# TensorE's order in the S5 part written out, with projection products between each unit's own

## The chip, the cores and the metric

The kernel runs on one core of a Trainium2 chip. Five engines work beside each other, each through its own queue and in order: TensorE (PE, with its weight loads PEld), VectorE (DVE), ScalarE (ACT), GpSimd (POOL) and SyncE (SP), which in this kernel issues nearly all DMAs. The metric is the device time of one execution in microseconds (us); the median of three executions of the kernel before is 683.53 us (682.38 to 684.18).

## The reference, cut to what matters

One layer over 1024 prompt tokens and 32 sample tokens (8 sequences of 4). The normalised input `a` is multiplied by `w_in`; the columns of the product feed an mLSTM group and an S5 group, whose outputs are joined, projected, and passed through two further stages of products.

```python
a = rmsnorm(h, ln_mix)
x_m, z_m, o_m, i_pre, f_pre, x_s, z_s = split(a @ w_in)   # 512 columns each, the gates 4 + 4
# mLSTM group: conv(x_m), q/k/v, gates i and f, chunkwise scan over the tokens, times sigmoid(o_m), silu(z_m)
# S5 group: 32 channel groups of 16 with a 64-dim complex diagonal state each
bu = einsum(x_s, Bbar); xs = associative_scan(a, bu)      # along the tokens
y  = Re(C xs) + D x_s;  y = gelu(y)
y  = y * sigmoid(y @ w_glu + b_glu) * silu(z_s)
h  = h + concat(hA, y) @ w_out
h  = h + sigmoid(h @ w_ple_gate) * rmsnorm(p @ w_ple);  out = rmsnorm(h, ln_final)
```

The change touches only the order in which `x_s`, `o_m`, `z_s` and the S5 units' products are made; what is computed stays the same.

## The kernel before, in words

All large products are made of three matmuls each (leading part times leading part, and two with a remainder: L116 to L118, in `mm3`). A projection of 128 columns of `w_in` over all 1056 tokens is `mtile`: for each of three token ranges (256, 384 and 416 tokens, `CH`) it runs 8 steps of three matmuls into one of two PSUM tiles of the tag `mm`, and then evacuates that tile. `s5_x(j, c)` does so for the j-th quarter of `x_s` (four quarters), and after the last range writes the quarter to DRAM (`d_us`, eight DMAs). `o_tile` does one token tile of `o_m` (8 steps of three 256-column matmuls); `o_rest` does the second half of `o_m`, which is eight such tiles and 64 small matmuls for the sample rows. `z_tile` is a projection for `z_m` or `z_s` with a tanh and a DVE product behind it, written to `d_z`. Weights come by `wtile`: a raw tile (two buffers), a leading part (three buffers) and a remainder (three), shared by all projections in the order of the program.

Order of the program: tokens are normalised and transposed, with the first half of `o_m` and quarter 0 of `x_s` between (up to 64 us of the profile); DVE prepares the S5 tables (L316 to L487); quarters 1 to 3 of `x_s`; then the eight S5 units, u = 0..7. A unit has two parts. `s5_mats(u)` prepares its matrices: DVE products `wtr`, `wti`; four transposes on TensorE (`tpW`, L514); the tile `WV`; `cs` from GpSimd products and DVE sums; four matmuls `kp` (L538); then `ks`, which goes to DRAM (`dK`) and comes back skewed as `tz`; and rotation tables on GpSimd. `s5_run(u)` runs it: the quarter's tokens `us` from `d_us`; eight matmuls `vr` and `vi` (L574) from `WV` and `us`; four products, two sums, four scans and six more products on DVE (L578 to L603), which give `xs_`; eight matmuls `py` (L609 from `tz` and `us`, L610 from `cs` and `xs_`); the GELU on ACT and DVE, with the result in `y2` and `ysm`; and eight DMAs of `y2` to `d_y`. After the units comes `s5_final`, and the buffers of the S5 part are closed (`s5x.close()`); the buffers of the mLSTM part are opened in the same place later. Then the mLSTM gates (a chain of small DVE operations, two transposes and four DMAs), the `x_m` projections with their convolution, the rest of `o_m`, the `z` projections and the four mLSTM heads, the GLU, and the output and gate products.

What sets the order: the engines take their queues in order, and the queues are laid out when the program is built, by a planner that goes through a simulated time. Of the instructions whose inputs are ready in that time it takes the one with the best priority; priority is the place in the program, and `tc.high_priority()` lifts it. In the kernel before all eight units stand in one `tc.high_priority()` block, so that a unit's products go ahead of any projection as soon as the planner sees them ready, and projections (also of later parts of the program) fill what is left, on every engine.

Of the kernel before, what the change touches and what calls it, by code (L numbers as in the profile page):

```python
# [8 lines left out]
F32 = mybir.dt.float32  # L9
# [14 lines left out]
CH = ((0, 256), (256, 384), (640, 416))  # L24
LOC = tuple((c, 128 * (i - b)) for i, (c, b) in enumerate(((0, 0),) * 2 + ((1, 2),) * 3 + ((2, 5),) * 4))
# [3 lines left out]
def tile_hymba(ctx: ExitStack, tc: tile.TileContext, d: dict, o: list):  # L29
# [27 lines left out]
    # ------------------------------------------------------------------ phase 1  # L57
# [67 lines left out]
    # ---------------- normalised input, transposed, in two parts  # L125
# [18 lines left out]
    def x_tile(i, xt):  # L144
# [8 lines left out]
        else:  # L153
            # the first tile in halves
# [19 lines left out]
    def mtile(hi, lo, evac, name, cs=(0, 1, 2)):  # L174
        for c in cs:
            t0, n = CH[c]
            ps = pm([128, 416], f"ps_{name}")
            for k in range(8):
                mm3(ps[:, :n], hi[:, k, :], lo[:, k, :], aTh[c][:, k, :n], aTl[c][:, k, :n], k == 0, k == 7)
            with tc.high_priority():  # L180
                evac(c, t0, n, ps)

    # ------------------------------------------------------------------ gates and output gate (token major)
# [15 lines left out]
    def o_tile(hh, ws, i):  # L199
        n = NH[hh]  # L200
# [3 lines left out]
        for k in range(8):  # L204
            hi, lo = ws[k // 4]
            mm3(ps[:m, :n], aTh[c][:, k, off:off + m], aTl[c][:, k, off:off + m],
                hi[:, k % 4, :], lo[:, k % 4, :], k == 0, k == 7)
        with tc.high_priority():
# [8 lines left out]
            if hh == 0:  # L217
                V.tensor_tensor(gates[:m, :, i], ps[:m, 256:264], bgr[:m], op=ADD)  # L218

    def o_rest():  # L220
        # the second half; its sample rows with the column blocks of w side by side in the array
# [12 lines left out]
        for j in range(4):  # L234
            p0 = 32 * (2 + j // 2)
            A.activation(sos[p0:p0 + 32, 64 * (j % 2):64 * (j % 2) + 64], ps[32 * j:32 * j + 32], AF.Tanh, scale=0.5)
        for i in range(8):
            o_tile(1, ws, i)
# [7 lines left out]
    def s5_x(j, c):  # L246
        if c == 0:
# [14 lines left out]
        mtile(*xsw[j], evac, "xs", (c,))  # L262
# [24 lines left out]
    # small parameters: rows -> columns by one transpose  # L287
# [26 lines left out]
    # ------------------------------------------------------------------ S5  # L314
# [44 lines left out]
    # bases e^{i theta 2^l}, l = 1..9, and rho = |a|^8  # L359
# [19 lines left out]
    # powers a^0 .. a^8 : [128, 16, 9]  # L379
# [12 lines left out]
    k = 1  # L392
# [4 lines left out]
    # rotation tables: fine A = E^1..E^8, coarse Bt = E^0, E^8, .., E^120 with E = e^{8 i theta}  # L397
# [16 lines left out]
    # input matrices times the ZOH factor  # L414
# [1053 lines left out]
```

## Time and profile before

| | |
|---|---|
| median of three timed executions | 683.53 us (682.38 to 684.18) |
| span of the profiled execution (first to last instruction) | 678.6 us |
| time of the profiled execution beyond its span | not given by the page |
| PE busy | 621.7 us, 92% of the span |
| DVE busy | 451.6 us, 67% |
| ACT, POOL busy | 252.2 us, 256.4 us |
| mean granted TensorE clock | 0.982 of full speed |
| chain that ended last, by engine | PE 56%, DVE 26%, DMA 6%, issue 5% |

The page gives busy time as a share of the whole span, so that 92% on PE is an average over stages with different limits. A busy time is the union of the instructions' own times; a matmul's time holds its way through the array (0.28 us for a product that the next one follows after 0.12 us), so that short waits between matmuls don't show as idle. The granted clock has two levels, 1.00 (2.4 GHz) and 0.50 (1.2 GHz); numbers between are means over a stretch.

### The profile page before, as it was taken

What the parts mean: (1) busy time and instruction counts of PE and PEld (TensorE: products, weight loads), DVE (VectorE), ACT (ScalarE), POOL (GpSimd) and SP (SyncE); (2) the same over time, 40 slices, a digit from 0 to 9 for tenths busy, and PEclk for the clock granted to TensorE, in tenths of its full rate; (3) what the DMA queues carried; (4) which work ended last, traced back from release to release, by engine and by line L of the source; (5) the groups of instructions that cost most, each with busy time, mean ns of one, the idle gap of its engine ahead of it and who ended that gap; (6) DMA issues with size and microseconds to landing.
All of it is one profiled execution on the core that took longest, in us unless ns stands there. A gap on an engine that the chain in (4) does not pass through costs nothing.

```text
span 678.6 us, 11611 instructions
## 1 busy us (share of the span) xinstructions
PE 621.7 (92%) x4068; PEld 543.6 (80%) x4068; DVE 451.6 (67%) x1257; ACT 252.2 (37%) x623; POOL 256.4 (38%) x269
## 2 busy tenths in 40 slices
PE   3998996987888897999999998999999999999995
PEld 2997995776767896899898978867888877788885
DVE  4779758999999966358678579966222324566435
ACT  5553331232232346314445253555111324443332
POOL 5712347665565126243533246583011203001000
PEclk9999998999979999999999998999999999999998
DMA  8804341153325366225345373577541246313111
GB/s 279 233 32 98 112 129 51 47 130 93 88 58 129 82 165 213 64 75 156 114 154 151 101 195 133 170 256 233 185 144 42 94 162 237 140 32 124 56 70 62
DMA packets 109679, 86.34 MB, mean 127 GB/s; under 512 B 33263, under 2 KB 92547, under 8 KB 109622
## 3 DMA queue, kind: packets, MB, share of 16 engines
q1 hardware_dynamic: 109622, 85.61, 41.9%
q8 instruction: 32, 0.52, 0.3%
q14 instruction: 25, 0.20, 0.1%
HBM read 60.10 MB, written 25.49 MB: 126 GB/s over the span
## 4 chain that ended last, share of the span: by engine, by line
PE 56%; DVE 26%; DMA 6%; issue 5%; ACT 3%; POOL 2%; SPq 1%; DVEq 0%; POOLq 0%; ACTq 0%
PE po L1287 5%; PE po L1289 4%; PE po L1288 4%; PE po L1396 4%; PE po L1398 4%; PE po L1397 4%; PE ps_zs L116 2%; PE ps_zs L117 2%; PE ps_zs L118 2%; DVE cs L533 2%; DVE cs L526 1%; SPq L35 1%; DVE zr L590 1%; DVE u L373 1%; PE pe L1377 1%
## 5 line engine op out<-in xcount | busy, mean ns | idle before, releaser
L1396 PE MATMUL po<-wgh,hTh 128*128 128x512 f32 (+1 forms) x136 | 52.1, 383 | 0.0
L1398 PE MATMUL po<-wgh,hTl 128*128 128x512 f32 (+1 forms) x136 | 51.5, 379 | 0.0
L1397 PE MATMUL po<-wgl,hTh 128*128 128x512 f32 (+1 forms) x136 | 51.4, 378 | 0.0
L116 PE MATMUL ps_o<-hi_o,aTh 128*128 128x264 f32 (+2 forms) x136 | 41.0, 302 | 0.7 <-ACT aTh L171 0.7
L117 PE MATMUL ps_o<-lo_o,aTh 128*128 128x264 f32 (+2 forms) x136 | 40.2, 296 | 1.4 <-POOL lo_o L112 1.4
L118 PE MATMUL ps_o<-hi_o,aTl 128*128 128x264 f32 (+2 forms) x136 | 40.4, 297 | 0.0
L116 PE MATMUL ps_xs<-aTh,hi_xs 128*128 128x256 f32 (+2 forms) x96 | 32.3, 337 | 2.5 <-DVE gates L218 2.5
L116 PE MATMUL ps_xm<-aTh,hi_xm 128*128 128x256 f32 (+2 forms) x96 | 33.8, 352 | 0.0
L116 PE MATMUL ps_zs<-aTh,hi_zs 128*128 128x256 f32 (+2 forms) x96 | 32.2, 335 | 0.7 <-DVE ztmp L666 0.7
L1287 PE MATMUL po<-woh,mh 128*128 128x512 f32 x80 | 32.6, 408 | 0.0
L117 PE MATMUL ps_xm<-aTl,hi_xm 128*128 128x256 f32 (+2 forms) x96 | 32.4, 338 | 0.0
L118 PE MATMUL ps_xs<-aTh,lo_xs 128*128 128x256 f32 (+2 forms) x96 | 32.1, 334 | 0.0
L118 PE MATMUL ps_zm<-aTh,lo_zm 128*128 128x256 f32 (+2 forms) x96 | 32.0, 334 | 0.0
L118 PE MATMUL ps_xm<-aTh,lo_xm 128*128 128x256 f32 (+2 forms) x96 | 32.0, 333 | 0.0
L117 PE MATMUL ps_xs<-aTl,hi_xs 128*128 128x256 f32 (+2 forms) x96 | 31.8, 332 | 0.0
L1288 PE MATMUL po<-wol,mh 128*128 128x512 f32 x80 | 31.8, 397 | 0.0
L118 PE MATMUL ps_zs<-aTh,lo_zs 128*128 128x256 f32 (+2 forms) x96 | 31.8, 331 | 0.0
L1289 PE MATMUL po<-woh,mlo 128*128 128x512 f32 x80 | 31.8, 397 | 0.0
L116 PE MATMUL ps_zm<-aTh,hi_zm 128*128 128x256 f32 (+2 forms) x96 | 31.7, 331 | 0.0
L117 PE MATMUL ps_zm<-aTl,hi_zm 128*128 128x256 f32 (+2 forms) x96 | 31.7, 330 | 0.0
L117 PE MATMUL ps_zs<-aTl,hi_zs 128*128 128x256 f32 (+2 forms) x96 | 31.5, 328 | 0.0
L1296 DVE TENSOR_TENSOR hTl<-tr,hTh 128x512 fp32r<-128x512 f32 x16 | 11.0, 690 | 30.3 <-ACT hTh L1295 30.1
(587 smaller groups left out, 2043.4 us busy)
## 6 DMA issues: line engine op xcount, KB each, us to landing
xt<-in_x_prompt SPq DMA_DIRECT2D x15, 512.0 KB
Wraw<-in_w_out SPq DMA_DIRECT2D x16, 256.0 KB
Wraw<-in_w_ple_gate SPq DMA_DIRECT2D x16, 256.0 KB
d_h<-xt SPq DMA_DIRECT2D x8, 512.0 KB
h_t<-d_h SPq DMA_DIRECT2D x8, 512.0 KB
out<-g_t SPq DMA_DIRECT2D x14, 256.0 KB
mt<-d_m SPq DMA_DIRECT2D x10, 256.0 KB
d_us<-xs SPq DMA_DIRECT2D x32, 72.0 KB
```

The costliest lines, as they stand in the source:

```text
L35: nc.sync.dma_start(out, in_)
L116: T.matmul(ps, wh, xh, start=first, stop=False)
L117: T.matmul(ps, wh, xl, start=False, stop=False)
L118: T.matmul(ps, wl, xh, start=False, stop=last)
L533: V.scalar_tensor_tensor(cs[64:128, g2:4:2], u1[ph], -1.0, u2[ph], op0=MUL, op1=SUB)
L1287: T.matmul(ps, mh[:, k % 4, :], hi, start=k == 4, stop=False)
L1288: T.matmul(ps, mh[:, k % 4, :], lo, start=False, stop=False)
L1289: T.matmul(ps, mlo[:, k % 4, :], hi, start=False, stop=k == 3)
L1296: V.tensor_tensor(hTl[i][:, 4 * q:4 * q + 4, :], tp, hi.bitcast(F32), op=SUB)
L1396: T.matmul(ps[:, :b - a], hTh[i][:, k, :], hi[:, ws], start=k == 4, stop=False)
L1397: T.matmul(ps[:, :b - a], hTh[i][:, k, :], lo[:, ws], start=False, stop=False)
L1398: T.matmul(ps[:, :b - a], hTl[i][:, k, :], hi[:, ws], start=False, stop=k == 3)
```

## The change

Inside the block `with tc.manual_schedule(engines={PE})` TensorE's instructions keep the order in which they are written; the other engines' queues are laid out as before. To write that order, the functions of the units and of the projections become generators that stop at given points. `take(cols)` runs on through `filler()`, which makes quarters 1 to 3 of `x_s`, then `o_rest`, then two of the four `z_s` projections, until so many matmul columns have been written (it stops at the first step boundary at or past the number). `prod` runs a unit's generator to its next stop, at high priority. `o_rest()` and `zs_tile(0)`, `zs_tile(1)` leave their old places behind the mLSTM gates. The order for each unit is: `vr`/`vi`, `kp`, 18,000 columns of filler, `py`, 2,400 columns, the next unit's `tpW`, 2,400 columns. The diff also drops comments.

```diff
+FILL_A, FILL_B, FILL_C = 18000, 2400, 2400
-    def mtile(hi, lo, evac, name, cs=(0, 1, 2)):
+    def mtile_g(hi, lo, evac, name, cs=(0, 1, 2)):
         for c in cs:
             t0, n = CH[c]
             ps = pm([128, 416], f"ps_{name}")
             for k in range(8):
                 mm3(ps[:, :n], hi[:, k, :], lo[:, k, :], aTh[c][:, k, :n], aTl[c][:, k, :n], k == 0, k == 7)
+                if k < 7:
+                    yield 3 * n
             with tc.high_priority():
                 evac(c, t0, n, ps)
+            yield 3 * n
...
     def o_rest():
...
+        yield 1200
         for i in range(8):
-            o_tile(1, ws, i)
+            yield from o_tile_g(1, ws, i)
...
     def s5_mats(u):
         cmul(V, wtr, wti, ...)
+        yield
         tp = pt([128, 4, 128], "tpW")
...
+        yield WV
         kp = pt([128, 128], "kp")
...
         cmul(G, rtr, rti, ...)
-        return WV, cs, tz, rtr, rti
+        yield cs, tz, rtr, rti
-    def s5_run(u, mats):
-        WV, cs, tz, rtr, rti = mats
+    def s5_run(u, WV, get):
...
                     T.matmul(v_[ph, q, :], WV[:, x, q, ph], us[:, 2 * q + g2, :], start=True, stop=True)
+        yield
+        cs, tz, rtr, rti = get()
...
         A.copy(fin[:, 2 * q0:2 * q0 + 4], xs_[:, :, 136])
+        yield
+        pys = []
         for q in range(2):
             ps = pn([128, 2, 136], "py")
+            pys.append(ps)
...
+        yield
+        for q, ps in enumerate(pys):
             sq = s5.tile([128, 2, 136], F32, tag="sq", name="sq", bufs=2)
...
-    for j in range(1, 4):
-        xsw.append(xs_w(j))
-        for c in range(3):
-            s5_x(j, c)
-    with tc.high_priority():
-        for u in range(8):
-            mats = s5_mats(u)
-            s5_run(u, mats)
-    s5_final()
-    s5x.close()
...
+    def filler():
+        for j in range(1, 4):
+            xsw.append(xs_w(j))
+            for c in range(3):
+                yield from s5_x_g(j, c)
+        yield from o_rest()
+        for j in range(2):
+            yield from z_tile_g(2056 + 128 * j, 4 + j, f"zs{j}")
+    fill = filler()
+    def take(cols):
+        for n in fill:
+            cols -= n
+            if cols <= 0:
+                break
+    def prod(gen):
+        with tc.high_priority():
+            return next(gen)
+    with tc.manual_schedule(engines={mybir.EngineType.PE}):
+        mats = [s5_mats(u) for u in range(8)]
+        prod(mats[0])
+        WV = prod(mats[0])
+        take(3000)
+        for u in range(8):
+            run = s5_run(u, WV, lambda: parts)
+            prod(run)
+            parts = prod(mats[u])
+            prod(run)
+            if u < 7:
+                prod(mats[u + 1])
+            take(FILL_A)
+            prod(run)
+            take(FILL_B)
+            if u < 7:
+                WV = prod(mats[u + 1])
+                take(FILL_C)
+            prod(run)
+        s5_final()
+        for _ in fill:
+            pass
+    s5x.close()
...
     xmc[0] = mtile_xm(0)
-    o_rest()
     xmc[1] = mtile_xm(1)
...
     zm_tile(1)
-    zs_tile(0)
-    zs_tile(1)
     glu_w()
```

## Rows read from the trace of the kernel before

**Rows 1.** Busy time by stretch: stretch, length, then busy us and instructions of each engine

```profile
core 0: us, PE busy (x) PEld busy (x) DVE busy (x) ACT busy (x) POOL busy (x), PEclk, DMA share, GB/s
63.70:94.90 31.20, 28.74 (x178) 28.13 (x176) 21.43 (x120) 11.53 (x35) 9.66 (x8) 0.95 0.46 133
94.90:232.90 138.00, 114.27 (x881) 98.94 (x879) 132.97 (x295) 36.57 (x120) 84.47 (x98) 0.95 0.34 85
232.90:300.00 67.10, 62.91 (x414) 59.40 (x415) 37.23 (x92) 27.31 (x60) 24.10 (x17) 1.00 0.48 132
300.00:445.00 145.00, 138.13 (x1018) 128.70 (x1018) 113.16 (x388) 66.81 (x169) 64.88 (x61) 0.99 0.48 147
445.00:678.60 233.60, 226.48 (x1223) 179.06 (x1222) 102.33 (x182) 77.32 (x182) 44.46 (x45) 0.99 0.38 129
```

**Rows 2.** Timeline of PE at 64 us: start, duration, instruction, idle before it

```profile
63.75 0.27 PE L460 MATMUL tpC<-ident,cn 128*128 128x128 f32 x1
66.59 0.39 PE L116 MATMUL ps_xs<-aTh,hi_xs 128*128 128x256 f32 x1 [2.46 <-DVE gates L218]
```

**Rows 3.** Timeline of DVE, the last table operation and the first unit's first two

```profile
79.61 0.29 DVE L377 TENSOR_TENSOR rBi<-cu,cu 128x128 f32<-128x128 f32 x1
89.83 0.40 DVE L372 TENSOR_TENSOR u<-pwr,Bbr 128x256 f32<-128x256 f32 x1
90.16 0.41 DVE L373 TENSOR_TENSOR u<-pwi,Bbi 128x256 f32<-128x256 f32 x1
```

**Rows 4.** Waits of DVE from 79 to 95 us: waiter, releaser, total, times, longest

```profile
DVE xs L249 <- DMA er<-ends: 4.0, 1, 4.0
DVE rw L711 <- PE tpr L710: 3.3, 1, 3.3
DVE M__2437 L731 <- DMA mp<-mc: 2.3, 1, 2.3
```

**Rows 5.** Timeline of PE around the first unit's products

```profile
103.08 0.43 PE L538 MATMUL kp<-cs,Bs 128*32 128x128 f32 x8
103.44 0.71 PE L574 MATMUL vr<-us,WV 128*64 128x144 f32 x8
104.57 0.46 PE L117 MATMUL ps_xs<-aTl,hi_xs 128*128 128x416 f32 x1
...
105.05 0.35 PE L116 MATMUL ps_xs<-aTh,hi_xs 128*128 128x416 f32 x1
105.24 0.35 PE L117 MATMUL ps_xs<-aTl,hi_xs 128*128 128x416 f32 x1
...
106.73 0.38 PE L514 MATMUL tpW<-ident,wtr 128*128 128x128 f32 x2
106.95 0.38 PE L514 MATMUL tpW<-ident,wti 128*128 128x128 f32 x2
```

**Rows 6.** Timeline of PE: half of unit 1's py, and unit 7's first and last products

```profile
138.90 0.47 PE L609 MATMUL py<-us,tz 128*128 128x136 f32 x2
139.90 0.38 PE L514 MATMUL tpW<-ident,wtr 128*128 128x128 f32 x2
214.46 0.70 PE L574 MATMUL vr<-us,WV 128*64 128x144 f32 x6
232.29 0.40 PE L610 MATMUL py<-xs__2316,cs 128*128 128x136 f32 x2
```

**Rows 7.** Groups of PE from 63.7 to 232.9 us, by line

```profile
L116 PE MATMUL ps_xm<-aTh,hi_xm 128*128 128x256 f32 (+2 forms) x48 | 17.0, 354 | 0.0
L116 PE MATMUL ps_zm<-aTh,hi_zm 128*128 128x256 f32 (+1 forms) x12 | 3.7, 308 | 0.0
L941 PE MATMUL vps<-wv,xm 128*128 128x128 f32 x16 | 2.1, 275 | 0.0
```

**Rows 8.** Busy time in stretches at the low and at the full clock

```profile
114.90:121.50 6.60, 5.91 (x36) 4.74 (x37) 6.59 (x17) 0.27 (x1) 4.12 (x5) 0.50 0.25 71
147.00:166.40 19.40, 13.96 (x117) 12.16 (x115) 19.12 (x38) 5.72 (x18) 11.49 (x14) 1.00 0.55 134
196.80:203.40 6.60, 6.60 (x33) 4.42 (x33) 6.60 (x7) 0.27 (x1) 6.60 (x5) 0.50 0.01 2
```

**Rows 9.** Waits of PE from 94 to 230 us

```profile
PE tps L754 <- DVE colv L746: 5.5, 1, 5.5
PE py L610 <- DVE xs__1676 L603: 2.9, 1, 2.9
```

**Rows 10.** Timeline of SP (DMA issues) in unit 6, and PE's wait for what they bring

```profile
204.46 3.83 SPq L35 DMA_DIRECT2D d_y<-y  x8
208.39 0.52 SPq L35 DMA_DIRECT2D dK<-ks  x1
210.98 0.62 SPq L35 DMA_DIRECT2D tz<-dK  x1
216.72 0.47 PE L609 MATMUL py<-us,tz 128*128 128x136 f32 x2 [1.56 <-DMA tz<-dK]
```

More of the change, by code (lines that the diff above doesn't have):

```diff
@@ L179, in mtile @@
                 mm3(ps[:, :n], hi[:, k, :], lo[:, k, :], aTh[c][:, k, :n], aTl[c][:, k, :n], k == 0, k == 7)
+                if k < 7:
+                    yield 3 * n
             with tc.high_priority():
                 evac(c, t0, n, ps)
+            yield 3 * n
+    def mtile(hi, lo, evac, name, cs=(0, 1, 2)):
+        for _ in mtile_g(hi, lo, evac, name, cs):
+            pass
     NH = (264, 256)
@@ L199, in o_tile, with o_tile_g @@
     def o_tile(hh, ws, i):
+        for _ in o_tile_g(hh, ws, i):
+            pass
+    def o_tile_g(hh, ws, i):
         n = NH[hh]
@@ L207, in o_tile @@
                 hi[:, k % 4, :], lo[:, k % 4, :], k == 0, k == 7)
+            if k < 7:
+                yield 3 * n
         with tc.high_priority():
@@ L218, in o_tile @@
                 V.tensor_tensor(gates[:m, :, i], ps[:m, 256:264], bgr[:m], op=ADD)
+        yield 3 * n
     def o_rest():
@@ L246, in s5_x, with s5_x_g @@
     def s5_x(j, c):
+        for _ in s5_x_g(j, c):
+            pass
+    def s5_x_g(j, c):
         if c == 0:
@@ L260, in evac @@
                 A.copy(xs[:, 4:8, 136:144], v)
-        mtile(*xsw[j], evac, "xs", (c,))
+        yield from mtile_g(*xsw[j], evac, "xs", (c,))
         if c == 2:
@@ L621, in s5_run @@
                 y2[16 * t:16 * t + 16].rearrange("c g (k n) -> c (g k) n", n=32))
+        yield
     def s5_final():
@@ L647, in s5_final, with z_tile_g @@
         dma(o_pim[0, 0], ob[:, 64:128])
-    for j in range(1, 4):
-        xsw.append(xs_w(j))
-        for c in range(3):
-            s5_x(j, c)
-    with tc.high_priority():
-        for u in range(8):
-            mats = s5_mats(u)
-            s5_run(u, mats)
-    s5_final()
-    s5x.close()
     def z_tile(c0, idx, name):
+        for _ in z_tile_g(c0, idx, name):
+            pass
+    def z_tile_g(c0, idx, name):
         hi, lo = wtile(wcols(c0, 128), 8, 128, name)
@@ L667, in evac @@
             dma(d_z[idx, :, t0:t0 + n], tz_[:, :n])
-        mtile(hi, lo, evac, name)
+        yield from mtile_g(hi, lo, evac, name)
+    def filler():
[36 more added lines that the diff above has]
+        for _ in fill:
+            pass
+    s5x.close()
     SC = 128.0 ** -0.5
```

## The prediction

> **What bounds the kernel now.** I read four views in this order. The busy times by stretch come first, because the change lies in one stretch: from 94.9 to 232.9 us, where the S5 units run, DVE is busy for 132.97 of 138.0 us and PE for 114.27; from 300 us on PE is at 95% or more [rows 1]. So the units' stretch is set by DVE, nearly all that follows by PE. The reader is to see that PE's 23.7 idle us there are the room that a better order can use, and that DVE's work is not made less by any order on PE. Second, PE's timeline at the units: the first unit's `vr` starts at 103.44, unit 7's at 214.46, and the last `py` ends at 232.7 [rows 5, 6]; that is (214.46 - 103.44) / 7 = 15.9 us a unit. Third, DVE's timeline ahead of the first unit: the S5 tables are finished at 79.9, but the first unit's products start at 89.83 [rows 3]; between 79 and 95 us DVE waits for 9.6 us in all, for a transpose and two small DMAs of the mLSTM gates, which stand in its queue ahead of the unit [rows 4]. Fourth, what PE does there: after a wait of 2.46 us it starts on quarter 1 of `x_s` at 66.59 [rows 2], and with quarters 1 to 3 it is busy for 28.7 of the 31.2 us up to 94.9 [rows 1].
>
> **The change, part by part.** Columns first: quarters 1 to 3 of `x_s` are 3 x 8 x 3 x 1056 = 76,032, `o_rest` counts 1,200 + 8 x 8 x 3 x 256 = 50,352, two `z_s` projections 50,688; together 177,072. At 0.19 us for 416 columns (105.05 to 105.24, [rows 5]), 0.457 ns each, that is 81 us of PE.
>
> *What is uncovered.* PE's written order begins with the first unit's `tpW`, which needs DVE's first products. The quarters that fill PE from 66.6 us today stand behind it, so PE has only a few transposes between 64 and about 82 us: some 16 us of idle PE. That costs nothing at once, as DVE works on the tables until 79.9; it takes 16 us out of PE's room, and those must come back in the units.
>
> *Start of the units.* Tables done at 79.9 [rows 3]; six products at 0.33 us apart (89.83 to 90.16, [rows 3]) 2.0; `tpW` 4 x 0.11 = 0.44 (106.73 to 106.95 for two, [rows 5]); `take(3000)` four steps, 3,072 columns, 1.4. PE comes out of a long idle; the 5.5 us wait for `colv` [rows 9] ended at the granted clock 0.50, which then held from 114.9 to 121.5 [rows 8], so I double the last two, 3.7. First `vr`: 79.9 + 2.0 + 3.7, some 86 with the hand-overs, against 103.4. Bounds: 84 at the full clock; 95.6 if the gates' 9.6 us of DVE waits come back ahead of the unit. I take 86: with `x_s` off PE and its `d_us` DMAs later, the transposes and DMAs of that chain have less ahead of them.
>
> *The period of a unit.* DVE alone: 15.9 us, as before. PE alone: 22,800 columns, and about half a step more at each of three stops (steps are 768 to 1,248 columns), say 24,300 x 0.457 = 11.1; `vr`/`vi` 1.13 (103.44 to 104.57), `kp` 0.36, `tpW` 0.44 [rows 5], `py` 2 x 1.0 (138.90 to 139.90, [rows 6]): 15.0. The two are nearly alike, and in a fixed order each waits for the other's lateness. The new wait is `py` behind 18,000 columns: queued behind `py` stand all the filler, `tpW` and the next `vr`, on which DVE depends. What `py` waits for is `xs_` and `tz`. `tz` comes by SP: eight `d_y` DMAs of the unit before, then `dK`, then `tz`: 204.46 to 208.39, 2.6 us until `tz` is issued, and PE has it 5.7 us after that [rows 10], 12.2 us in all. If that chain starts with `vr`, `py` runs at 12.2, and the next `vr` comes 2.0 + 1.3 + 0.44 + 1.3 = 5.0 us later (two blocks of about 2,900 columns): 17.2. Ends: 15.9 (DVE alone; `tz` early) and 19.7 (the chain 2.5 us late). I take 17.0, nearest to the row of the chain. New DVE work in this stretch, the six evacuations of `z_s`, leaves the stretch that follows by as much and is inside the 1.1 us over 15.9.
>
> *The last unit.* 18.2 us before, from `vr` to the end of `py` [rows 6]. The filler lasts (177,072 - 3,072) / 24,300 = 7.2 units, so unit 7 has little beside it; with 12.2 for `tz`, 2.0 for `py` and a little for `xs_`, 15. Ends 13 and 18.
>
> *End of the units:* 86 + 7 x 17.0 + 15 = 220, against 232.7: 12.7 us earlier.
>
> *What is left for later.* `z_s` 0 and 1 take the place of `x_m` 0 and 1, 48 steps each [rows 7], the same columns. Not done by then, and done before: 12 steps of `z_m` (36 matmuls, some 10,800 columns, 4.9 us) and 16 `vps` [rows 7], 2.1 us at 0.13 each: 7 us of PE. Against it unit 7 leaves PE about 9 us free, in which the projection `x_m` 0 may start, as it is outside the written order, if its weights are there; I count 3. Net 4 us later, ends 0 and 7. After that the same work is queued: ten projections (9.6 before) to lay beside four mLSTM heads, on a PE that is 94% to 97% busy [rows 1]; I take it at the same pace.
>
> *Sum:* -12.7 + 4 = -8.7 us on the span of 678.6, 669.9. The median of the runs is 4.9 us above that span (the page gives no other time for the profiled execution); I carry this over: 674.8, say 675.
>
> **A rule of the skill against it.** The rows show both: the 5.5 us wait [rows 9] was followed by the clock 0.50 [rows 8], the 2.9 us wait in unit 2 [rows 9] was not: 147.0 to 166.4 ran at 1.00 [rows 8]. The Trainium skill, "TensorE: Matmul & The Clock Gate", section "HAM oscillation — how this bites in real kernels", says that a loop whose every pass waits for a transfer between its bursts of matmuls starts every pass at the low clock. [...] It is the first rival.
>
> **The rivals.** *Low clock in each unit.* If every unit loses the clock for 6.6 us, as at 114.9 and 196.8 [rows 8], PE needs 15.0 + 3.3 = 18.3 a unit and sets the period: 86 + 128 + 15 = 229, -3.6 + 4: 684, no change. For it: PE waits in each unit by my own period. Against: these waits are 2 us, and the trace's 2.9 us cost no clock. The page named above has this as a rule; the price is the rows' alone.
>
> *`tz` rules, and it is late (slower).* The written order fixes `py` 18,000 columns after `kp`, 8.2 us; before, PE took other work until `tz` came. If `ks` or the `d_y` DMAs ahead of it on SP are 2.5 us later than I count, the period is 19.5: 86 + 136.5 + 15 = 237.5, +4.8 + 4 us: 692. It decides from a period of 18.2 us on, where the sum is zero: 86 + 7 x 18.2 + 15 + 4 = 232.4. For it: unit 6 waited for `tz` even with 18 us between `kp` and `py`. Against: in that unit `d_y` stood behind other work; in the new order `y2` comes right after `py`.
>
> *The gates stay ahead on DVE.* The first `vr` comes at 95.6, and the change gives 684: PE's 16 idle us are then lost, and the units end only 3 us earlier. For it: the planner put them there before [rows 4]. Against: its reason, a DVE free while PE was full, is mostly gone.
>
> *More than I count.* If the units keep the DVE period of 15.9, unit 7 takes 13 and nothing is left over: 86 + 111.3 + 13 = 210.3, -22.4 us: 661. For it: DVE is at 96% already in a looser order. Against: PE at 15.0 leaves it no slack.
>
> **How the numbers follow.** Forecast (period 16.2 to 17.8, 669 to 681): 0.43. More: 0.17. Low clock: 0.11. `tz` late: 0.22. Gates ahead: 0.07, about half of it no change and half slower. A change of 0.3%, 2.1 us, is what a measurement of this kernel can tell from none. Faster 0.43 + 0.17 = 0.60, same 0.11 + 0.03 = 0.14, slower 0.26. The range reaches from near the best case to the late `tz`: 662 to 691; the forecast's own is 669 to 681.
>
> **What would show it.** Right: PE idle from 64 to about 82 us; the first `vr` near 86; `vr` to `vr` 17 us; PE's waits in the units small and named `tz` or `xs_`, the granted clock 1.00 after the first unit; `tpf` near 220; beyond it the stretches of the kernel before, shifted. Wrong: a first `vr` past 95, a period past 18.2, a clock of 0.50 in most units, or more idle PE between the end of the units and 445 us than the 11 us of before.

## The result, and the profile after

The changed kernel takes 706.14 us (704.65 to 709.0, 4 runs) against 682.95 us (681.86 to 684.18) of the kernel before beside it: a ratio of 1.035 [1.032, 1.038]. It is slower, where 675 us (662 to 691) was forecast. Its profiled execution has a span of 704.0 us (678.6 before) and a mean clock of 0.953 (0.982 before).

The busy times by stretch, of the kernel before and then of the changed one, are cut at the first `vr` and at `tpf`, the first transpose behind unit 7 (columns as in [rows 1]):

```profile
62.00:103.44 41.44, 38.98 (x241) 37.60 (x239) 30.23 (x140) 14.60 (x42) 18.06 (x16) 0.96 0.43 122
103.44:232.91 129.47, 105.73 (x830) 91.16 (x826) 125.89 (x287) 34.85 (x116) 76.62 (x90) 0.95 0.34 86
232.91:678.60 445.69, 427.53 (x2652) 367.16 (x2652) 252.70 (x660) 171.43 (x409) 133.44 (x121) 0.99 0.43 135
```

```profile
62.00:87.72 25.72, 7.80 (x32) 5.32 (x30) 24.67 (x126) 8.39 (x27) 9.72 (x11) 0.62 0.45 126
87.72:255.66 167.94, 136.80 (x1026) 128.60 (x1026) 136.21 (x296) 41.60 (x127) 87.94 (x94) 0.90 0.32 81
255.66:704.00 448.34, 429.51 (x2659) 368.80 (x2657) 251.44 (x658) 171.41 (x411) 135.03 (x121) 0.99 0.42 133
```

The first unit starts at 87.72, 15.7 us earlier [rows 5]; unit 7 ends 22.7 us later, at 255.66; what follows is 2.6 us longer. So the units lost 38.5 us: their eight `vr` stand at 87.72, 112.12, 136.51, 154.25, 174.52, 197.22, 218.78 and 243.97, 22.3 us apart in the mean (15.9 before). In this stretch DVE, busy for all but 3.6 us before, is now idle for 31.7 us and PE for 31.1 (23.7 before). Neither is full: the two wait for each other. The third line of both says how little the rest has to do with it.

What PE waits for from 60 to 260 us, and DVE from 85 to 256 us (waiter, releaser, total us, times, longest):

```profile
PE py L636 <- DMA tz<-dK: 13.9, 5, 4.3
PE tpr L780 <- DVE gin L775: 10.5, 1, 10.5
PE ps_zs L117 <- DVE ztmp L689: 9.7, 2, 5.3
PE vr L596 <- ACT xs L280: 3.5, 1, 3.5
PE py L637 <- DVE xs__1153 L627: 3.0, 1, 3.0
```

```profile
DVE sq L643 <- ACT sq L642: 12.6, 8, 3.7
DVE ztmp L689 <- ACT ztmp L688: 5.8, 2, 5.1
DVE w L602 <- PE vr L596: 3.5, 1, 3.5
DVE cs L548 <- PE py L637: 3.4, 4, 1.0
```

The 10.5 us lie ahead of the units; the waits of before in them are [rows 9]. In the units PE's largest wait is the forecast one, `py` for `tz`, in five of the eight; the second is that of a `z_s` product for its evacuation (`ztmp`), 9.7 us in units 5 and 6. DVE's largest is `sq`, the first operation behind `py`, in all eight (its releaser, ACT's square, waits for `py` itself). Unit 4 shows the circle, first on PE, then on DVE, then on SP:

```profile
174.52 0.71 PE L596 MATMUL vr<-us,WV 128*64 128x144 f32 x8 [0.21 <-ACT WV L538]
175.65 0.43 PE L561 MATMUL kp<-cs,Bs 128*32 128x128 f32 x8
189.22 0.79 PE L636 MATMUL py<-us,tz 128*128 128x136 f32 x2 [4.29 <-DMA tz<-dK]
195.06 0.38 PE L536 MATMUL tpW<-ident,wtr 128*128 128x128 f32 x2
197.22 0.71 PE L596 MATMUL vr<-us,WV 128*64 128x144 f32 x8
```

```profile
173.95 2.58 DVE L397 TENSOR_TENSOR u<-pwi,Bbr 128x256 f32<-128x256 f32 x1
176.56 0.92 DVE L555 SCALAR_TENSOR_TENSOR cs<-u,u 64x288 f32<-64x288 f32 x2
...
180.67 0.41 DVE L604 TENSOR_TENSOR w<-vi,rtr 128x256 f32<-128x256 f32 x1
181.00 0.51 DVE L565 SCALAR_TENSOR_TENSOR ks<-dsel,Dt,ks 128x16 f32<-128x16 f32 x1
...
187.29 0.87 DVE L627 TENSOR_TENSOR xs__2085<-v,v 64x256 f32<-64x256 f32 x2
191.84 0.44 DVE L643 SCALAR_TENSOR_TENSOR sq<-sq,py 128x272 f32<-128x272 f32 x1 [3.68 <-ACT sq L642]
```

```profile
177.96 3.06 SPq L36 DMA_DIRECT2D d_y<-y  x6
181.12 0.41 SPq L36 DMA_DIRECT2D d_so<-sot  x1
181.62 0.55 SPq L36 DMA_DIRECT2D dK<-ks  x1
182.22 0.95 SPq L36 DMA_DIRECT2D d_y<-y  x2
184.08 0.62 SPq L36 DMA_DIRECT2D tz<-dK  x1
```

`kp` is written at 175.65, but `ks` comes on DVE only at 181.00, behind this unit's `w` and the next unit's `u` and `wti`; `dK` follows at 181.62, `tz` is issued at 184.08, 2.5 us later, and PE has it 5.1 us after that. PE has run out of its 18,000 columns 4.29 us before. Meanwhile DVE has finished `xs_` and waits 3.68 us for `py`; then come 2,400 columns, `tpW`, 2,400 columns, and only then the next `vr`. In the kernel before the next `vr` did not stand behind `py`; in five of the seven cases it came 1.0 to 3.8 us ahead of it, as `vr` of unit 2 and `py` of unit 1 do here:

```profile
132.17 0.70 PE L574 MATMUL vr<-us,WV 128*64 128x144 f32 x6
135.88 0.47 PE L609 MATMUL py<-us,tz 128*128 128x136 f32 x2 [1.21 <-issue]
```

In the changed kernel it comes 5.0 to 10.2 us behind the start of `py`, in all seven. The low clock (0.50) covers 35.0 of the 167.9 us of the units: 0.9 us at their start and seven pieces of 3.4 or 6.8 us behind it; one of these, 187.6 to 194.4, begins inside this very wait.

### The profile page after: what moved, and what is told of

Same layout as the page of the kernel before. It is cut to its first block, busy times and chain, and to the rows that moved or that the text cites. A ratio compares the mean times of both kernels' runs of the same rounds, so it can differ in the third digit from the quotient of the medians.

```text
span 704.0 us, 11593 instructions
## 1 busy us (share of the span) xinstructions
PE 623.0 (88%) x4068; PEld 549.3 (78%) x4068; DVE 456.3 (65%) x1257; ACT 253.4 (36%) x623; POOL 261.5 (37%) x269
## 4 chain that ended last, share of the span: by engine, by line
PE 57%; DVE 23%; DMA 10%; issue 4%; ACT 3%; SPq 1%; POOL 1%; POOLq 0%; DVEq 0%; ACTq 0%
PE po L1354 4%; PE po L1356 4%; PE po L1355 4%; PE po L1463 4%; PE po L1465 4%; PE po L1464 4%; DMA tz<-dK 2%; PE ps_xm L117 2%; PE ps_xm L119 2%; PE ps_xm L118 2%; PE ps_zs L117 2%; DMA raw_o<-in_w_in 2%; PE ps_zs L119 1%; PE ps_zs L118 1%; SPq L36 1%
```

## The experiments

Three theories at first, A, B and C. **A**: the written order makes each unit a closed round trip (`vr`, DVE, `ks`, `dK`, `tz`, `py`, DVE, `tpW`, `vr`), in which PE and DVE take turns. **B**: the projections' evacuations, moved into the units, hold DVE and ACT. **C**: the low clock is the loss. Later came **A2** (A, with DVE's order as the longer half, not the DMAs), **D** (it is the fixed order itself, wherever it waits), **A3** (`vr` of the next unit stands behind `py`), **L** (a ledger of PE's idle time over the whole kernel) with its counterpart **E** (the end of the units sets the time), and **D2** (DVE sets the units once the loop is open). All runs are in one table. Each ratio is to the kernel before as it was timed beside the run, whose median was 682.63 to 684.86 us, so that two medians of different rows compare only to some 2 us. The columns are read from windows cut at the first `vr` and at `tpf`, as above. "PE idle" is counted from 62 us on, ahead of the units, in them, and behind them.

| run | median us | ratio to before | first `vr` | `tpf` | PE idle us | DVE idle in units |
|---|---|---|---|---|---|---|
| before | 682.95 | | 103.4 | 232.9 | 2.5 + 23.7 + 18.2 | 3.6 |
| after | 706.14 | 1.035 | 87.7 | 255.7 | 17.9 + 31.1 + 18.8 | 31.7 |
| e1 planner | 687.98 | 1.004 | 102.7 | 240.5 | 2.5 + 19.9 + 18.0 | 8.8 |
| e2 24,000 | 696.14 | 1.016 | 87.8 | 251.9 | 17.9 + 16.4 + 26.4 | 27.2 |
| e3 one block | 702.38 | 1.025 | 87.0 | 250.0 | 17.7 + 30.4 + 15.0 | 24.9 |
| e4 mats ahead | 684.71 | 1.000 | 88.1 | 234.1 | 18.2 + 13.8 + 19.5 | 19.7 |
| e5 e4, cover | 692.64 | 1.011 | 92.5 | 235.6 | 6.9 + 22.7 + 24.6 | 14.2 |
| e6 cover only | 716.28 | 1.046 | 90.6 | 257.4 | 6.0 + 39.4 + 23.4 | 32.7 |
| e7 no `z_s` | 708.51 | 1.036 | 88.2 | 248.5 | 17.9 + 24.6 + 27.0 | 25.8 |
| e8 old `tz` | 702.36 | 1.027 | 86.8 | 250.8 | 17.9 + 28.6 + 18.3 | 28.2 |
| e10 `py` behind `vr` | 712.66 | 1.042 | 88.3 | 264.3 | 17.9 + 35.2 + 20.1 | 39.3 |
| e9 two units | 696.20 | 1.019 | 89.9 | 235.2 | 18.1 + 15.2 + 24.0 | 16.9 |
| e11 e9, cover | 681.26 | 0.996 | 92.0 | 232.2 | 6.1 + 23.6 + 15.9 | 7.9 |
| e12 e9, fewer columns | 711.26 | 1.041 | 89.1 | 234.8 | 18.3 + 26.1 + 25.4 | 16.3 |
| e13 e11, `kp` later | 676.80 | 0.991 | 91.5 | 225.7 | 6.2 + 22.2 + 15.1 | 3.9 |
| e14 e11, half cover | 694.24 | 1.017 | 89.8 | 224.5 | 11.3 + 19.0 + 22.4 | 5.5 |
| e15 e13, planner | 689.21 | 1.007 | 102.3 | 236.9 | 2.5 + 20.1 + 19.2 | 5.9 |
| e16 e13, `kp` later still | 679.64 | 0.994 | 94.0 | 227.4 | 5.6 + 19.1 + 16.6 | 2.5 |

**e1, the planner's order for the same program.**

```diff
-    with tc.manual_schedule(engines={mybir.EngineType.PE}):
+    with ExitStack():
```

> The changed kernel's program, with the filler and the generators in their new places, but without the written order on TensorE: the planner lays out PE's queue as on the other engines. Theory A (the fixed order makes each unit wait for tz, which is sent only after kp and lands some 14 us after vr): without it PE takes other work until tz is there, the period from vr to vr falls from 22.3 us to 16 to 17, and the time lies near the kernel before, 675 to 690. Theory B (moving o_rest and two z_s projections into the S5 part is what costs, since their evacuations stand on DVE and ACT): the period stays above 20 us and the time above 698.

687.98 us, 1.004 [1.001, 1.006]. The written order itself accounts for 18 to 20 of the 23 us; what is moved (`x_s`, `o_rest`, `z_s`) for some 3 to 5. The period is 16.8 us here, and the low clock covers 30.7 us of these units, little less than in the changed kernel.

**e2, more columns ahead of `py`; e3, all columns in one block ahead of it.**

```diff
-FILL_A, FILL_B, FILL_C = 18000, 2400, 2400
+FILL_A, FILL_B, FILL_C = 24000, 2400, 2400      # e2
+FILL_A, FILL_B, FILL_C = 22800, 0, 0            # e3
...
     def take(cols):
+        if not cols:                             # e3
+            return
```

> 24,000 instead of 18,000 columns between kp and py, 2.7 us more PE work ahead of the wait for tz. Theory A (the loop from kp by ks, dK and tz to py and on to the next kp sets the period): the waits for tz shrink to below 1 us in most units and with them the falls of the clock, the period of units 0 to 4 stays within 2 us of 22.3 at the same work per clock, or falls to 20 to 21 by the clock alone; time 698 to 706. Theory C (the granted clock's fall after each wait is the main loss, the loop itself is short): with PE busy through the waits the clock stays at 1.00 and the period falls below 19.5 us; time below 692.

> All 22,800 columns of a unit stand between kp and py, none between py, tpW and the next vr. Theory A: the loop loses the two blocks of 2,400 columns (2.6 us at the full clock, up to 5 at the half), py starts when tz is there or up to 1 us later: period 18 to 20 us, time 688 to 697. Theory C: PE has the longer block as cover for tz, no fall of the clock, period below 18 us, time below 688. Theory B: no change, 701 to 710.

e2: 696.14, 1.016 [1.013, 1.019]. The waits for `tz` fall to 4.5 us and the low clock in the units from 35.0 to 15.7 us, yet the period is still 21.8. With the low clock near that of the kernel before (13.7 us), 10 to 12 of the 23 us went. As 6,000 columns a unit came in with it, the period alone doesn't settle C; together with e1, which has the low clock and not the period, C is refuted as the main cause. e3: 702.38, 1.025 [1.021, 1.028]: the waits for `tz` fall to 8.6 us, but `py` now waits 10.6 us for `xs_`, in six waits, and `vr` 4.2 us for `WV`, in seven. A's figure (688 to 697) missed.

**e4, the matrices one unit ahead.** `tpW`, `cs`, `kp`, `ks`, `dK` and `tz` of unit u + 1 in the middle of unit u's columns; `vr` of u + 1 still behind `py` of u.

```diff
+        nxt = prod(mats[0])
         for u in range(8):
+            parts = nxt
             run = s5_run(u, WV, lambda: parts)
             prod(run)
-            parts = prod(mats[u])
             prod(run)
             if u < 7:
                 prod(mats[u + 1])
-            take(FILL_A)
-            prod(run)
-            take(FILL_B)
+            take(FILL_A // 2)
             if u < 7:
                 WV = prod(mats[u + 1])
                 take(FILL_C)
+                nxt = prod(mats[u + 1])
+            take(FILL_A // 2)
+            prod(run)
+            take(FILL_B)
             prod(run)
```

> Each unit's matrices one unit earlier in the written order: tpW, cs, kp and so ks, dK and tz of unit u+1 stand in the middle of the 18,000 columns of unit u, ahead of py of unit u. Theory A: the wait for tz is gone and DVE's products for the next unit no longer stand between py and the next vr; the period falls to DVE's 16 to 17 us, the end of the units to 220 to 226 and the time to 675 to 685. Theory B (evacuations of the filler): period above 20 us, time above 698. Theory C: as A in sign, but less than half of it, since every other wait still lowers the clock: 690 to 698.

684.71, 1.000 [0.998, 1.002]: by the ratio all 23 us are back (by the medians 21), by one edit. The stretch of its units, and the group of `py` from `tz` in the changed kernel and in this one (busy, mean ns, idle before it):

```profile
88.05:234.10 146.05, 132.23 (x1025) 123.24 (x1023) 126.36 (x297) 41.82 (x128) 77.35 (x93) 0.94 0.38 96
```

```profile
L636 PE MATMUL py<-us,tz 128*128 128x136 f32 x64 | 17.5, 367 | 13.9 <-DMA tz<-dK 13.9
```

```profile
L636 PE MATMUL py<-us,tz 128*128 128x136 f32 x64 | 13.6, 296 | 0.6 <-DVE zi L614 0.6
```

The wait for `tz` is gone, and PE's idle time in the units is 13.8 us. But the period is 19.0, not A's 16 to 17. PE is now the fuller of the two, busy for 132.2 us in eight units, 16.5 each (DVE 15.8); `vr` still stands behind the `py` of the unit before, and DVE waits 13.9 us with `sq` for `py`. Which of the two keeps the period at 19.0, the run does not show.

**e5 and e6, the hole ahead of the first unit filled**, in e4 and in the changed kernel alone; the columns beside each unit are fewer by about as much.

```diff
-FILL_A, FILL_B, FILL_C = 18000, 2400, 2400
+FILL_A, FILL_B, FILL_C = 14000, 1800, 1800
         prod(mats[0])
+        take(34000)
         WV = prod(mats[0])
```

> As the run with the matrices one unit earlier, and 34,000 columns of the filler (quarter 1 of x_s and a part of quarter 2) written ahead of the first unit's tpW, with 14,000, 1,800 and 1,800 columns in the units. Theory A (the loop over tz is the loss, the uncovered 20 us ahead of the units a second one that the units' room does not give back): PE works from 64 to 82 us, does not come out of the wait at the low clock, the units have 5,000 columns less each; first vr 85 to 88, period 16.5 to 18, the end of the units at 218 to 226 us, time 668 to 678. Rival (the units are set by DVE and PE has room to spare, so that the uncovered stretch was free): the end and the time as in the run before, 681 to 687.

> The changed kernel's unit order with the same 34,000 columns ahead of the first tpW and 14,000, 1,800 and 1,800 in the units. Theory A: with only 6.4 us of columns between kp and py the wait for tz is longer in each unit (4 to 7 us), the loop and with it the period stay at 20 to 22 us; the end of the units moves by less than 8 us, time 696 to 708. Rival (the uncovered 20 us are the loss and the waits for tz only fill what PE has too little work for): the end moves earlier by 12 us and more, time below 692.

e5: 692.64, 1.011 [1.007, 1.014]; e6: 716.28, 1.046 [1.042, 1.049]. Both missed, and upwards; some 7 us of each lie in the last stage of the kernel, which PE takes in another order there (see e9). In e6 the hole shrinks from 17.9 to 6.0 us, but PE's idle time in the units grows from 31.1 to 39.4, as `py` waits for `tz` six times, 24.1 us in all, with fewer columns to spend the round trip on; the units take 166.8 us with a quarter fewer columns, 167.9 in the changed kernel. So long as the loop is closed, columns put elsewhere only turn into waits.

**e7, `z_s` back in its old place.**

```diff
         yield from o_rest()
-        for j in range(2):
-            yield from z_tile_g(2056 + 128 * j, 4 + j, f"zs{j}")
...
+    zs_tile(0)
+    zs_tile(1)
```

> The changed kernel with the two z_s projections back behind the mLSTM gates, so that the filler ends with o_rest. Theory A: units 0 to 4 as in the changed kernel, 21 to 23 us each; units 5 and 6 lose their waits for the evacuation tile ztmp (9.7 us) but still wait for tz; the end of the units 8 to 16 us earlier, and half or more of that given back by the z_s projections later: time 696 to 704. Theory B (evacuations of the filler on DVE and ACT are the loss): the units' period falls to 18, time below 692.

708.51, 1.036 [1.032, 1.040]. The units end 7.2 us earlier, the rest is 11 us longer (6.7 of them in the last stage, see e9), and the time is the same. The period is 20.9 us: B is refuted as the main cause, but 1.4 us of the 22.3 go with the `z_s` projections.

**e8, `py` with the `tz` of the unit before.**

```diff
+    tzs = [None]
...
         cs, tz, rtr, rti = get()
+        tz, tzs[0] = tzs[0] or tz, tz
```

This leaves out the wait for the fresh `tz`; what `py` computes is then something else.

> The changed kernel, but py of unit u reads the tz of unit u-1 (unit 0 its own), which leaves the S5 output with other kernels; every instruction stays in its written place and only the wait for the fresh tz goes. Theory A in its narrow form (the DMA chain ks, dK, tz is what py waits for): the waits for tz vanish, period 17 to 19, time 685 to 693. Theory A2 (the written order puts DVE's products wtr, wti and cs of the next unit between py and the next kp, and that, not the DMA, closes the loop): py waits for xs_ instead, period 20 us and more, time 698 to 706.

702.36, 1.027 [1.023, 1.031]; the waits for `tz` are 3.6 us, the period 21.8. So the wait for the DMAs alone is worth 4 to 5 us, and the narrow form of A fell. A2's figures held: `py` waits 6.5 us for `xs_` (3.0 in the changed kernel). That DVE, on which `cs` and the other products of the matrices stand between `vr` and `py`, closes the round trip instead is in part argued: 10.3 us of PE's waits here are for `ztmp` and 4.5 for `us` from `d_us`, which lie outside it. e4 moves the matrices' work on DVE out of that way too, and with it `tpW` and one block of 2,400 columns to a place ahead of `py`.

**e10, `py` behind the next `vr`, nothing else; e9, the same in e4's order.** The lines of the edit that matter, with comments put in:

```diff
...
+                runs[u + 1] = s5_run(u + 1, WV, lambda n=u + 1: held[n])
+                prod(runs[u + 1])          # vr(u+1)
+            prod(runs[u])                  # py(u)
...
```

> One edit on the changed kernel: py of unit u stands behind vr of unit u+1 (kp(u), 18,000 columns, tpW(u+1), 2,400, vr(u+1), py(u), 2,400). Theory A3 (in the kernel before, vr of the next unit stands ahead of or beside py of this one on PE, so that two units overlap on DVE; the written order closes a loop py -> DVE -> tpW -> vr -> DVE -> py in which DVE and PE take turns): DVE has the next unit's w products while py, its sq and its evacuation run; the period of a unit falls from 22.3 us to 16.5 to 18.5, the waits for tz fall under 5 us in all, and the time is 675 to 692. Rival A2 (the round trip of one unit, vr - xs_ - ks - dK - tz - py, is too long in any fixed order with these columns, wherever py stands): the period stays at 20 or more and the time at 697 to 710. Rival D (what a fixed order loses is that it cannot take other PE work at a wait, wherever the wait is): the waits move to vr, the period stays over 20, and the clock still falls in most units: 697 or more.

> The kernel with the matrices one unit ahead (684.7 us, period 19.0) with vr of unit u+1 put ahead of py of unit u as well. Theory A3: in that kernel the loop py -> sq -> next vr was still closed, which is why the period stayed at 19 with the waits for tz gone; with two units in flight DVE sets the period, 15.9 to 17.2 us, the first vr at 88 and tpf at 213 to 222, so 664 to 676 us. Rival A2: tz was already early there, so nothing changes: 682 to 688. Rival D (each wait of a fixed order costs the clock, wherever it is): period 18 or more, 680 to 690.

e10: 712.66, 1.042 [1.038, 1.045]; e9: 696.20, 1.019 [1.016, 1.022]. A3 is refuted as the cause: letting `vr` overtake `py` gives nothing in either order (e11 below shows a gain of it beside the cover). PE's largest waits in e10's units:

```profile
PE ps_zs L117 <- DVE ztmp L689: 10.4, 2, 5.5
PE vr L596 <- ACT WV L538: 5.9, 1, 5.9
PE vr L596 <- DMA us<-d_us: 5.6, 1, 5.6
PE py L636 <- DMA tz<-dK: 4.7, 2, 3.1
```

In unit 2 `kp` stood at 146.89, behind the `py` of unit 1, and its own `py` came at 162.55, 15.7 us later and behind a wait of 3.14 us for `tz`: `kp`, `ks`, `dK`, `tz`, `py` and the next `kp` still form a loop. But the waits for `tz` are 4.7 us in all, so that this loop is only a part of e10's loss; the rest is not traced. In e9 that loop is open too, and its units end within 1.1 us of e4's; it is 11 us slower for what comes behind them, 7 of them in the last stage. That stage, from `tpsh` to the end, of e4 and then of e9:

```profile
438.02:682.90 244.88, 235.64 (x1317) 186.51 (x1315) 109.49 (x215) 84.13 (x196) 51.38 (x52) 0.99 0.40 131
```

```profile
441.88:693.90 252.02, 238.21 (x1314) 187.28 (x1312) 111.00 (x214) 82.55 (x193) 52.22 (x51) 0.98 0.38 127
```

This stretch lies far behind the edit and holds nearly the same products, but the planner lays it out in more than one way. In eleven kernels (before, after, e1, e3, e4, e8, e10, e11, e12, e13, e15) PE's order there is the same, product for product, and takes 243 to 246 us; in e5, e6, e9 and e14 it is another, all but the same in these four, of 251 to 252 us; e7 has one of its own of 251, e2 and e16 of 242 and 246. So some 7 us in the times of e5, e6, e7, e9 and e14 belong to no theory of the units; why the planner falls into one or the other stays open.

**e11, e9 with the hole filled (e5's edit).**

> The same with 34,000 columns of xs ahead of the first tpW and 14,000/1,800/1,800 beside each unit, so that PE's 16 idle us between 64 and 82 us are filled. Theory A3: with the loop open the columns beside each unit are what PE has too much of; with a quarter fewer, PE alone needs 12 us a unit and DVE's 15.9 sets it; but the first vr is later by up to 5 us (92.5 in the earlier run with this cover), and the columns done ahead come off later work: 660 to 674 us. Rival (the columns that run ahead of the first unit delay its start by as much as they save, as in the earlier run with the matrices ahead, which lost 8 us by it): 3 to 9 us over the run without the cover.

681.26, 0.996 [0.994, 0.998]: slightly faster than before, though slower than A3 expected. PE's idle time is 6.1 us ahead and 23.6 in the units, DVE's there 7.9. e5 is this kernel but for `vr` ahead of `py`: its units took 143.1 us and DVE idled 14.2 of them, here 140.2 and 7.9. So beside the cover A3's edit is worth some 3 us of the units; of the 11 us between the two times 8.6 lie in the last stage.

**e12, e9 with the fewer columns of e11 but no cover; e13, e11 with 3,800 columns between `tpW` and `kp`; e14, e11 with half the cover.**

```diff
+FILL_A, FILL_B, FILL_C = 14000, 1800, 1800      # e12, on e9
+FILL_A, FILL_B, FILL_C = 12000, 1800, 3800      # e13, on e11
+        take(17000)                             # e14, on e11, for take(34000)
```

> The order of the run with two units (696.2 us; units from 89.9 to 235.2) with 14,000/1,800/1,800 columns instead of 18,000/2,400/2,400 beside each unit and no cover ahead of the first; the columns that are left run behind unit 7. Theory L (a ledger of PE: from 62 us on PE was busy for 568 to 586 us in every run so far, so the time is that sum and PE's idle time, wherever it lies; the end of the units does not set it): the units end earlier, 222 to 230 us, since PE alone needs less there, but the hole of 18 idle us before the first unit stays, the idle time in the units is 18 to 26 us, and the columns come later: 682 to 697 us. Rival E (the end of the units sets the time, as the prediction summed it): the end of the units moves by 5 to 13 us and the time with it, to 671 to 681 us if what follows takes the 446 us of the kernel before.

> The best version so far (681.3 us; cover of 34,000 columns, matrices ahead, vr of the next unit ahead of py) with 3,800 instead of 1,800 columns between tpW and kp and 12,000 instead of 14,000 in the two other blocks: kp waited for WV and cs for 10.1 of the 23.6 idle us of PE in its units. Theory L: up to 8 of these us are filled with columns, and the time falls by as much as PE's idle total does: 672 to 679 us. Rival D2 (DVE sets the units there, with 7.9 us idle in 140, so that the wait only moves to vr or py): PE's idle time in the units stays at 20 to 25 us and the time at 679 to 685.

> The best version so far with a cover of 17,000 instead of 34,000 columns. Theory L: PE is idle for 7 to 9 us more in the hole; the first vr comes at 88 to 90 instead of 92; the units' idle time is 20 to 24 us as DVE sets them; the columns come back later: 1 to 8 us slower, 682 to 689. Rival E (the end of the units sets the time): the units end 2 to 4 us earlier and so does the kernel: 676 to 680.

e13: 676.80, 0.991 [0.989, 0.994], faster than both kernels. `kp` waits for 4.8 instead of 10.1 us, and the units take 134.2 instead of 140.2; PE's idle time in them falls only from 23.6 to 22.2. e14: 694.24, 1.017 [1.014, 1.020]. e12: 711.26, 1.041 [1.038, 1.044]. Both were 5 us and more above L's ranges, e13 within; e14 carries the 7 us of the last stage, and without them it would lie inside. The stretches of e13 and of e14:

```profile
62.00:91.48 29.48, 23.27 (x141) 21.22 (x139) 25.01 (x126) 10.29 (x31) 13.44 (x14) 0.90 0.45 130
91.48:225.66 134.18, 111.96 (x894) 103.08 (x892) 130.26 (x297) 38.49 (x121) 76.49 (x92) 0.92 0.38 95
225.66:673.40 447.74, 432.62 (x2682) 371.98 (x2680) 249.65 (x657) 172.24 (x413) 134.07 (x121) 0.99 0.42 133
```

```profile
62.00:89.84 27.84, 16.50 (x91) 13.49 (x90) 26.13 (x126) 9.12 (x28) 11.18 (x13) 0.82 0.41 116
89.84:224.48 134.64, 115.60 (x908) 106.69 (x906) 129.17 (x298) 38.25 (x121) 78.22 (x92) 0.92 0.40 98
224.48:692.50 468.02, 445.66 (x2718) 380.16 (x2716) 250.32 (x655) 173.25 (x415) 137.78 (x122) 0.98 0.40 128
```

Their units end 1.2 us apart, e14's first, and both 7 to 8 us ahead of the kernel before; their times are 17 us apart. E is refuted: an early end of the units does not set the time by itself. e14 has left PE more to do: by then 43 steps of `z_s` and 2 of `x_m` are done, in e13 48 and 9 to 10. These 12 to 13 steps, of some 1,056 columns at 0.457 ns each, are 6 us, and the last stage has 7.8 more (250.95 against 243.20 us); 6 to 7 of the 20.3 us by which what follows the units is longer in e14 are not traced. e12 ends its units 5 to 13 us later than both thought: one unit took 33.7 us, of which PE spent 15 on a chain of the mLSTM gates' small matmuls (`tpv` at 125.58 to `gps` at 135.59, and a wait of 4.4 us ahead of it), which the planner had put between the written ones. It leaves half of `z_s` and all of `x_m`, 40 steps or 19 us more than e9 leaves; its units end where e9's do, and the stretch from there to the last stage is 24 us longer. L is in part a ledger that can't fail, busy time plus idle time; what it claims beyond that, that the busy time stays, held only to 18 us (568 to 586 us from 62 us on).

**e15, e13 under the planner; e16, 5,400 columns ahead of `kp`.**

```diff
+    with ExitStack():                           # e15, on e13
+FILL_A, FILL_B, FILL_C = 10400, 1800, 5400      # e16, on e13
```

> The best version so far (676.8 us) with its written order on TensorE taken away: the same program in the same order of emission, but the planner lays out PE's queue. If the written order itself is what gains (theory L: DVE's idle time in the units, 3.9 us there against 20 to 39 us in the other written orders, and a PE that never stands before a unit's products): 681 to 692 us, PE idle in all 45 to 58 us. Rival (the gain lies in what is moved, the projections of x_s, o and z_s beside and ahead of the units, and a planner finds the same order): 673 to 680 us. In the changed kernel the written order cost 18 us against the planner's.

> The best version so far with 5,400 instead of 3,800 columns between tpW and kp and 10,400 instead of 12,000 in the two other blocks. kp still waited for WV and cs for 4.8 us there, py for xs_ for about 7: theory L: what kp no longer waits comes as a wait of py, whose vr now stands nearer; PE's idle time in the units stays at 20 to 25 us: 674 to 681 us. Rival (kp's waits were the limit still): 4 us less idle time, 670 to 674.

e15: 689.21, 1.007 [1.004, 1.009]: of e13's program, the written order gains 11 to 12 us over the planner's, the same thing that lost 18 to 20 in the changed kernel. So D, that a fixed order loses wherever it waits, is refuted as a rule. PE's idle time is no less in e15 (41.8 us in all against 43.6); its busy time is more, 583.7 against 567.9 us from 62 us on. PE was busy for 35.5 us at the clock of 0.50 (26.8 in e13); half of the difference, 4 us, is an estimate from these of what the clock explains, and the rest is not explained. What the expectation gave as a mark of e13, DVE's idle time of 3.9 us against 20 to 39 in the other written orders, is none: e14 has 5.5 us and e11 7.9. e16: 679.64, 0.994 [0.992, 0.996], no better than e13. `kp` waits for 6.2 us there, more than the 4.8 of e13, so the edit did not take away the waits that it was aimed at, and whether they were still the limit is not shown. DVE is idle for 2.5 us of 133, so that DVE sets the units, which D2 had thought of e13 already.

## Why the prediction was wrong

*The failed step is the period of a unit: 17.0 us forecast, 22.3 measured.* Seven periods too long by 5.3 us are 37 us; the sum of the other terms is off by 6 us the other way. The step had two halves. From `vr` to `py` it counted 12.2 us and the trace has 14.7 in the mean (12.5 to 18.3); from `py` to the next `vr` 5.0, and the trace has 7.6 (5.0 to 10.2). The prediction had the mechanism as its second rival, `tz` late in a written order, and priced it at 19.5 from a single delay of 2.5 us. The row that gave the right size was quoted and used for something else: in the kernel before, unit 7, which no other unit follows, takes 18.2 us from `vr` to the end of `py` [rows 6], the others 21.5 to 26.3, but the units follow each other by 15.9. They overlap. An order that closes the loop makes latency into period: 18.2 plus two blocks and `tpW`, about 3 us, is 21. In hindsight that reading gives 86 + 7 x 21 + 15 = 248, and 703 us in all. e8 and e4 show that to take the wait for `tz` out of the loop is not enough, and that to take all of the matrices' work out of it, DVE's included, is. A smaller part was put at nearly nothing: the evacuations of `z_s`, which the sum had inside 1.1 us a unit of DVE's time, held PE for 9.7 us (`ztmp`), and without `z_s` the period is 20.9 (e7).

*What it named as the chain.* "If that chain starts with `vr`": it did, but `ks` stands in DVE's queue behind work of two units (unit 4: 5.4 us from `kp` to `ks`), where the prediction counted only SP. Its argument against the late `tz`, that `d_y` comes right after `py`, did not hold: unit 3's `py` starts at 167.04, its `y` comes on DVE at 177.51, and six of its eight `d_y` go out at 177.96, 3.4 us into unit 4 and ahead of its `dK`. In the row for it, unit 6 of the kernel before, `kp` stands at 196.79, 20 us ahead of `py`, not 18.

*PE alone, 15.0 us:* e4 has 16.5 busy us a unit. Part of this is the low clock, 17.1 us of e4's units; the prediction left it out of the sum although [rows 8] had it in the kernel before.

*The uncovered stretch, 16 us:* right; 17.9 idle us against 2.5. "Those must come back in the units" was right as a condition, and the sum did not keep to it: at a period of 17.0 PE would still have been idle for 2 us a unit. e4 has just that, 13.8 us idle in the units, and is no faster than before; but its period is 19.0. e13, with a period of 17.2 and units that end 7.3 us earlier than before, is 5.2 us shorter, and it has the hole filled. So whether the forecast of 8.7 us gained would have come with its period is not shown.

*Start of the first unit, 86:* 87.72, right; the gates did not stay ahead on DVE. *Last unit, 15:* 11.7, below its bounds. *Left for later, +4:* +2.6, near, but in part by luck: the sum counted 3 us of `x_m` done by then, and PE had done 16 steps, 7.6 us, since the units ended late. *From span to median, +4.9:* +2.1.

*The first rival, the clock.* In the units it fell seven times, in six of the eight, with or right behind waits of PE of 1.8 to 5.3 us, and was low for 35.0 us in all. The Trainium skill, "TensorE: Matmul & The Clock Gate", section "HAM oscillation — how this bites in real kernels", says that in a loop that waits for a transfer in each pass every pass starts at the low clock. The trace agrees in part: four of the seven falls go with a wait for `tz`, three with a wait for an evacuation. The two waits that the prediction set side by side, 5.5 us with a fall and 2.9 without, do not tell when the clock falls: the fall at 196.8 [rows 8] came right behind a wait of 1.85 us, which it did not trace. But the low clock came with the waits and is not the main cause of the period: e2 removed more than half of it and was still 11 to 13 us slower than before, and e1 kept 30.7 us of it with a period of 16.8.

*Range and chances.* The upper end, 691, stood on the 19.5; no case priced a fully closed loop, so 706 lay outside.

## What to carry to other kernels

Before writing out one engine's order for units in a loop, compare in the trace the latency of one unit with the distance between units: where latency is larger, the units overlap, and every instruction that the new order puts behind a later step of the same unit must be checked for a loop; its latency becomes the period. Open the loop by making what depends on nothing in the unit (here its matrices) one unit ahead, and only then tune how much filler stands where: with the loop closed, no amount or place of filler that was tried got below 696 us; with it open, the same knobs decided between 677 and 711. And where one engine is nearly full over the whole kernel, judge an order by that engine's idle and busy time over the whole kernel and the work that it leaves, not by when the stretch ends: two kernels whose units ended within 1.2 us of each other were 17 us apart. Look also at the stages far behind an edit before giving a difference to it: 8 of these 17 us come from another layout of the last stage.

## What the runs showed of the hardware

DVE's time in the units is not a constant. The changed kernel and e4 run 296 and 297 DVE instructions there, in 136.2 and 126.4 busy us. One operation of unit 4, `u<-pwi,Bbr` (L397), took 2.58 us (above); its mean is 1.03 us in the changed kernel and 0.42 in e4. Beside it POOL was at a weight remainder of `z_s`, for nearly the same time:

```profile
173.74 2.52 POOL L113 TENSOR_TENSOR lo_zs<-raw_zs,hi_zs 128x1024 fp32r<-128x1024 f32 x1 [0.44 <-ACT hi_zs L112]
```

The two rows ended 0.3 us apart. This is not one case: in the units of before, after, e4 and e13, all 128 DVE products of this form (`TENSOR_TENSOR`, 128x256, f32) that took over 0.45 us had POOL's work beside them and ended within 0.4 us of the end of a POOL instruction; of the 152 with none beside them not one took over 0.43 us. Not every product with POOL beside it is slow, and no run took POOL's work away, so that the one holds up the other is likely and not tested.
